# A prefix log-sum-exp scan: seven of eight batches in a hardware loop, four tile buffers, and a last tile loaded whole

## Chip, cores and metric

The kernel runs on one core of one Trainium2 chip. The metric is the device time of one execution in microseconds (us). A profile of one execution comes with it; its span goes from the first to the last instruction and is a little shorter than the device time.

## What is computed

The input is float32 of shape 8 x 4096 x 2048: eight batches, 4096 positions, 2048 channels. Along the positions each output is the running log of the sum of exponentials:

```
out[:, 0, :] = x[:, 0, :]
for t in range(1, S):
    mx = maximum(out[:, t-1, :], x[:, t, :])
    out[:, t, :] = mx + log(exp(out[:, t-1, :] - mx) + exp(x[:, t, :] - mx))
```

The kernel computes it as the log of a running sum of exp(x), without the maximum. Each batch is a scan of its own.

## The kernel before

A tile is 512 positions of one batch with all 2048 channels, 4 MiB; eight tiles (k = 0 to 7) make a batch, 64 the whole input. Partition p of a tile holds four successive positions (r = 0 to 3), and these lie one after the other in memory, so that the tile is 32 KiB in a row for each of the 128 partitions, in one DMA (L76). A tile is worked on in four pieces of 512 channels (c = 0 to 3). Python loops write all 256 pieces out; there is no branch in the program.

For each piece `front` has the ScalarE engine (ACT) take Exp of all four positions into bf16 (L88). Four matmuls with triangular masks sum over partitions into a PSUM bank (L91). VectorE (DVE) copies the bank (L96) and adds the positions r = 1 to 3 one after the other (L98); the result is `st`. `carry` multiplies the last row of `st` with the mask `last`, and so puts the running total of the tile into the bank of the next tile of the same batch (L103). `back` takes Ln of `st`, on ACT, and writes it over the input in the tile's buffer (L110). After the fourth piece the tile leaves in one DMA, issued by ACT (L114).

The order on each engine is the order in which the code is written: front of piece n, carry of piece n-1, back of piece n-2 (LAG = 2). So on ACT the last two Ln of a tile, and its store behind them, stand behind the first two Exp of the next tile, across batches too. Loads are issued by the SP queue, stores by the ACT queue. The pool `iopool` has five buffers for tiles (L52). A load is written ahead of all work of its tile, and it waits on SP until the store of the tile that had the buffer before has landed.

The last of the 64 tiles is an exception: it is loaded in four DMAs, one per piece (L74), each with 2 KiB in a row, and stored in four (L112). The masks are made at the start by GpSimd (POOL).

Of the kernel before, what the change touches and what calls it, by code (L numbers as in the profile page):

```python
# [1 line left out]

# [4 lines left out]


@with_exitstack
def kernel(  # L10
    ctx: ExitStack,
    tc: tile.TileContext,
    x: bass.AP,
    out: bass.AP,
):

    nc = tc.nc
    f32 = mybir.dt.float32
    bf16 = mybir.dt.bfloat16
    ACT = mybir.ActivationFunctionType
    nc.scalar.preload_act_table_set("natural_log_exp_and_others")  # L29

    B, S, D = x.shape
    P = 128
    R = 4
    NBLK = S // (P * R)
    FD = 512
    NC = D // FD
    LAG = 2

    const = ctx.enter_context(tc.tile_pool(name="const", bufs=1))
    Li = const.tile([P, P], bf16)  # L40
    masks.make_upper_triangular(nc, Li, val=1.0, diag=True)
    Ls = const.tile([P, P], bf16)
    masks.make_upper_triangular(nc, Ls, val=1.0, diag=False)

    last = const.tile([P, P], f32)
    nc.gpsimd.memset(last, 1.0)  # L46
    nc.gpsimd.affine_select(  # L47
        out=last, in_=last, compare_op=mybir.AluOpType.is_ge, fill=0.0,
        base=-(P - 1), pattern=[[0, P]], channel_multiplier=1,
    )  # L50

    iopool = ctx.enter_context(tc.tile_pool(name="iopool", bufs=5))  # L52
    epool = ctx.enter_context(tc.tile_pool(name="epool", bufs=4))
    spool = ctx.enter_context(tc.tile_pool(name="spool", bufs=3))
    ppool = ctx.enter_context(tc.tile_pool(name="ppool", bufs=2, space=bass.MemoryType.PSUM))

    x_v = x.rearrange("b (k p r) d -> b k p r d", p=P, r=R)
    o_v = out.rearrange("b (k p r) d -> b k p r d", p=P, r=R)

    tiles = [(b, k) for b in range(B) for k in range(NBLK)]  # L60
    pieces = [(b, k, c) for b, k in tiles for c in range(NC)]
    io = {}
    sums = {}
    banks = {}

    def cols(c):
        return slice(c * FD, (c + 1) * FD)

    def load(b, k):
        t = iopool.tile([P, R, D], f32, name=f"io_{b}_{k}", tag="io")  # L70
        io[b, k] = t
        if (b, k) == tiles[-1]:
            for c in range(NC):
                nc.sync.dma_start(out=t[:, :, cols(c)], in_=x_v[b, k][:, :, cols(c)])  # L74
        else:
            nc.sync.dma_start(out=t, in_=x_v[b, k])  # L76

    def bank(b, k, c):
        if (b, k, c) not in banks:
            banks[b, k, c] = ppool.tile([P, FD], f32, name=f"ps_{b}_{k}_{c}", tag=f"ps{c}")  # L80
        return banks[b, k, c]

    def front(b, k, c):
        if c == 0:
            load(b, k)
        t = io[b, k]
        et = epool.tile([P, R, FD], bf16, name="et")
        nc.scalar.activation(et, t[:, :, cols(c)], ACT.Exp)  # L88
        ps = bank(b, k, c)
        for r in range(R):  # L90
            nc.tensor.matmul(  # L91
                ps, Li if r == 0 else Ls, et[:, r, :],
                start=(k == 0 and r == 0), stop=(r == R - 1), skip_group_check=True,
            )
        st = spool.tile([P, R, FD], f32, name="st")
        nc.vector.tensor_copy(st[:, 0, :], ps)  # L96
        for r in range(1, R):
            nc.vector.tensor_add(st[:, r, :], st[:, r - 1, :], et[:, r, :])  # L98
        sums[b, k, c] = st

    def carry(b, k, c):
        if k < NBLK - 1:
            nc.tensor.matmul(  # L103
                bank(b, k + 1, c), last, sums[b, k, c][:, R - 1, :],
                start=True, stop=False, skip_group_check=True,
            )

    def back(b, k, c):
        t = io[b, k]
        nc.scalar.activation(t[:, :, cols(c)], sums.pop((b, k, c)), ACT.Ln)  # L110
        if (b, k) == tiles[-1]:
            nc.scalar.dma_start(out=o_v[b, k][:, :, cols(c)], in_=t[:, :, cols(c)])  # L112
        elif c == NC - 1:
            nc.scalar.dma_start(out=o_v[b, k], in_=t)  # L114

    for n, piece in enumerate(pieces):
        front(*piece)
        if n >= 1:
            carry(*pieces[n - 1])
        if n >= LAG:  # L120
            back(*pieces[n - LAG])
    for piece in pieces[-LAG:]:
        back(*piece)


# [1 line left out]
_INS = ['x']  # L127
_OUTS = [((8, 4096, 2048), 'float32')]


# [23 lines left out]
```

## Time and profile before

| What | Value |
|---|---|
| Time, median of 10 runs | 1259.64 us (1259.51 to 1259.86) |
| The profiled execution's own time | 1259.65 us |
| Its span | 1257.9 us |
| ACT busy | 930.0 us (74%), 513 instructions |
| DVE busy | 703.6 us (56%) |
| TensorE busy | 643.7 us (51%) |
| DMA | 537.22 MB, mean 427 GB/s over the span |
| HBM read and written | 268.44 MB each |

The profile's page gives the span in 40 slices of equal length. In them a digit is the busy share of an engine in tenths, and a number is the rate of all 16 DMA engines of the core in GB/s. A group line has: line, engine, operation, tiles written and read, shapes and count; then its busy time and the mean duration of one in ns; then the idle time of the engine just before such instructions and what ended it. A DMA line ends with the size of one DMA and the median time from issue to landing. In the queue's own waits, the three numbers are the time in total, how often, and the longest.

### The profile page before, as it was taken

The page shows a single profiled execution, that of the slowest core. Times are in us where ns is not written, and L with a number is a line of the kernel's source. Part 1 is how long each engine was busy: PE and PEld are TensorE (multiplying, and loading weights), DVE is VectorE, ACT ScalarE, POOL GpSimd, SP SyncE. Part 2 cuts the span into 40 slices and gives each one's busy share as a digit, 9 for nine tenths or more (in the row PEclk, how much of TensorE's full clock was granted, in tenths as well). Part 3 has the DMA queues.
Part 4 walks back from the last instruction along what each step waited for, and adds up shares of the span by engine and source line. Part 5 has one row for each costly group of instructions (what it writes and reads, how often), then busy time and mean ns, then how long its engine had stood idle before and what let it go on. Part 6 is the DMA issues. An engine that isn't in the chain of part 4 may idle for free.

```text
span 1257.9 us, 5492 instructions
## 1 busy us (share of the span) xinstructions
PE 643.7 (51%) x1472; PEld 215.9 (17%) x1472; DVE 703.6 (56%) x1024; ACT 930.0 (74%) x513; POOL 1.5 (0%) x10
## 2 busy tenths in 40 slices
PE   4655446554555455554555545455555455454542
PEld 1211112111111111111111111111111111111110
DVE  3766556555565554655555656565465555655453
ACT  5987768668677686776867768678687686776665
POOL 0000000000000000000000000000000000000000
PEclk9888577776787857878578786787767877678695
DMA  9999999999999999999999999999999999999997
GB/s 401 426 431 433 433 432 430 432 432 434 433 434 432 431 433 432 433 431 433 432 433 433 432 433 433 433 433 433 434 432 433 434 433 431 433 433 433 433 382 299
DMA packets 22399, 537.22 MB, mean 427 GB/s; under 512 B 2144, under 2 KB 2144, under 8 KB 6240
## 3 DMA queue, kind: packets, MB, share of 16 engines
q1 hardware_dynamic: 11184, 268.44, 49.7%
q10 hardware_dynamic: 11184, 268.44, 49.6%
q8 instruction: 11, 0.18, 0.1%
q14 instruction: 20, 0.16, 0.0%
HBM read 268.44 MB, written 268.44 MB: 427 GB/s over the span
## 4 chain that ended last, share of the span: by engine, by line
DMA 72%; ACT 15%; issue 5%; DVE 3%; PE 3%; SPq 1%; ACTq 0%; DVEq 0%
DMA io<-in_x_dram 69%; ACT io L110 9%; ACT et L88 6%; DVE st L98 2%; DMA out_dram<-io 2%; PE ps L91 2%; PE ps L103 1%; DVE st L96 1%; SPq L74 1%; ACTq L114 0%; ACTq L110 0%; ACTq L88 0%; DVEq L98 0%; DVEq L96 0%; SPq L76 0%
## 5 line engine op out<-in xcount | busy, mean ns | idle before, releaser
L88 ACT ACTIVATE et<-io 128x2048 bf16<-128x2048 f32 x256 | 485.3, 1897 | 302.9 <-DMA io<-in_x_dram 302.9
L98 DVE TENSOR_TENSOR st<-st,et 128x512 f32<-128x512 f32 x768 | 531.0, 692 | 43.4
L110 ACT ACTIVATE io<-st 128x2048 f32<-128x2048 f32 x256 | 484.6, 1894 | 13.3 <-DMA io<-in_x_dram 10.7
L96 DVE COPY st<-ps 128x512 f32<-128x512 f32 x256 | 176.8, 690 | 498.0 <-PE ps L91 492.9
L103 PE MATMUL ps<-st,last 128*128 128x512 f32 x448 | 309.0, 779 | 135.6 <-DVE st L98 134.5
L91 PE MATMUL ps<-et,Li 128*128 128x512 bf16 x256 | 125.7, 491 | 462.7 <-ACT et L88 461.1
L91 PE MATMUL ps<-et,Ls 128*128 128x512 bf16 x768 | 288.2, 498 | 0.0
L91 PEld LDWEIGHTS <-Ls 128*128 128x128 bf16 x768 | 89.7, 117 | 695.2 <-issue 666.1
L103 PEld LDWEIGHTS ps<-st,last 128*128 128x128 f32 x448 | 95.1, 237 | 250.2 <-DVE st L98 227.7
L91 PEld LDWEIGHTS <-Li 128*128 128x128 bf16 x256 | 31.1, 121 | 79.7 <-issue 72.7
L29 ACT ACT_TABLE_LOAD x1 | 1.3, 1283 | 0.8 <-PEq L138 0.8
L47 POOL TENSOR_SCALAR_AFFINE_SELECT last<-last 128x128 f32<-128x128 f32 x1 | 0.3, 292 | 0.1
masks.py:66 POOL TENSOR_SCALAR_AFFINE_SELECT Li<-Li 128x128 bf16<-128x128 bf16 x1 | 0.3, 292 | 0.0
masks.py:66 POOL TENSOR_SCALAR_AFFINE_SELECT Ls<-Ls 128x128 bf16<-128x128 bf16 x1 | 0.3, 292 | 0.0
masks.py:65 POOL MEMSET Li<- 128x128 bf16 x1 | 0.2, 204 | 0.3 <-POOLq L138 0.3
masks.py:65 POOL MEMSET Ls<- 128x128 bf16 x1 | 0.2, 204 | 0.0
L46 POOL MEMSET last<- 128x128 f32 x1 | 0.2, 204 | 0.0
L138 POOL MEMSET const-bfloat16-1.0<- 128x1 bf16 x1 | 0.1, 102 | 0.0
L138 POOL MEMSET const-uint8-127<- 128x1 uint8 x1 | 0.1, 102 | 0.0
L138 POOL MEMSET const-float32-0.0<- 128x1 f32 x1 | 0.1, 98 | 0.3 <-issue 0.3
L138 POOL MEMSET const-float32-1.0<- 128x1 f32 x1 | 0.1, 98 | 0.0
## 6 DMA issues: line engine op xcount, KB each, us to landing
io<-in_x_dram SPq DMA_DIRECT2D x63, 4096.0 KB, 31.4
out_dram<-io ACTq DMA_DIRECT2D x63, 4096.0 KB, 38.5
io<-in_x_dram SPq DMA_DIRECT2D x4, 1024.0 KB, 39.5
out_dram<-io ACTq DMA_DIRECT2D x4, 1024.0 KB, 10.3
```

The costliest lines, as they stand in the source:

```text
L29: nc.scalar.preload_act_table_set("natural_log_exp_and_others")
L46: nc.gpsimd.memset(last, 1.0)
L47: nc.gpsimd.affine_select(out=last, in_=last, compare_op=mybir.AluOpType.is_ge, fill=0.0, base=-(P - 1), pattern=[[0, P]], channel_multipl ...
L74: nc.sync.dma_start(out=t[:, :, cols(c)], in_=x_v[b, k][:, :, cols(c)])
L88: nc.scalar.activation(et, t[:, :, cols(c)], ACT.Exp)
L91: nc.tensor.matmul(ps, Li if r == 0 else Ls, et[:, r, :], start=(k == 0 and r == 0), stop=(r == R - 1), skip_group_check=True,)
L96: nc.vector.tensor_copy(st[:, 0, :], ps)
L98: nc.vector.tensor_add(st[:, r, :], st[:, r - 1, :], et[:, r, :])
L103: nc.tensor.matmul(bank(b, k + 1, c), last, sums[b, k, c][:, R - 1, :], start=True, stop=False, skip_group_check=True,)
L110: nc.scalar.activation(t[:, :, cols(c)], sums.pop((b, k, c)), ACT.Ln)
L138: nc = _bacc.Bacc("TRN2", target_bir_lowering=False, num_devices=1)
```

## The change

Batches one to seven become the body of a hardware loop, `tc.For_i(0, B - 1, 1, iteration_sync="reg_based")`; batch eight is written out after it. The body is one batch, eight tiles written out as before, and the batch's number comes from a register, in the DRAM address of every load and store. The loop construct, by its own description, does not reset its semaphores between iterations: they only increase, and a wait in the body compares with a register that is raised at each iteration. The semaphores belong to the loop alone; they are raised by one iteration's ticks ahead of it and cleared in its exit block.

The pieces of one batch are now a list of their own: the last two `back` of a batch come at its end and no longer behind the first two `front` of the next batch. The pool of tile buffers has four instead of five. The last tile is loaded by the same DMA as every other. Its results leave in three DMAs: channels 0 to 1023 after the second piece, then one per piece. Exp, matmuls, sums and Ln are the same. The diff, cut to its core:

```diff
-    iopool = ctx.enter_context(tc.tile_pool(name="iopool", bufs=5))
+    iopool = ctx.enter_context(tc.tile_pool(name="iopool", bufs=4))
...
-    def load(b, k):
-        t = iopool.tile([P, R, D], f32, name=f"io_{b}_{k}", tag="io")
-        io[b, k] = t
-        if (b, k) == tiles[-1]:
-            for c in range(NC):
-                nc.sync.dma_start(out=t[:, :, cols(c)], in_=x_v[b, k][:, :, cols(c)])
-        else:
-            nc.sync.dma_start(out=t, in_=x_v[b, k])
...
+    def batch(b, final):
+        pieces = [(k, c) for k in range(NBLK) for c in range(NC)]
+        io, sums, banks = {}, {}, {}
+        xb = x_v[b] if isinstance(b, int) else x_v[bass.ds(b, 1)][0]
+        ob = o_v[b] if isinstance(b, int) else o_v[bass.ds(b, 1)][0]
...
+        def front(k, c):
+            if c == 0:
+                io[k] = iopool.tile([P, R, D], f32, name=f"io{k}", tag="io")
+                nc.sync.dma_start(out=io[k], in_=xb[k])
...
+        def back(k, c):
+            nc.scalar.activation(io[k][:, :, cols(c)], sums.pop((k, c)), ACT.Ln)
+            if final and k == NBLK - 1:
+                if c > 0:
+                    part = slice(0 if c == 1 else c * FD, (c + 1) * FD)
+                    nc.scalar.dma_start(out=ob[k][:, :, part], in_=io[k][:, :, part])
+            elif c == NC - 1:
+                nc.scalar.dma_start(out=ob[k], in_=io[k])
+
+        for n, piece in enumerate(pieces):
+            front(*piece)
+            if n >= 1:
+                carry(*pieces[n - 1])
+            if n >= LAG:
+                back(*pieces[n - LAG])
+        for piece in pieces[-LAG:]:
+            back(*piece)
+
+    with tc.For_i(0, B - 1, 1, iteration_sync="reg_based") as b:
+        batch(b, False)
+    batch(B - 1, True)
```

More of the change, by code (lines that the diff above doesn't have):

```diff
@@ L58 @@
     o_v = out.rearrange("b (k p r) d -> b k p r d", p=P, r=R)
[L60 to L64, printed above, removed]
     def cols(c):
         return slice(c * FD, (c + 1) * FD)
-    def load(b, k):
-        t = iopool.tile([P, R, D], f32, name=f"io_{b}_{k}", tag="io")
-        io[b, k] = t
-        if (b, k) == tiles[-1]:
-            for c in range(NC):
-                nc.sync.dma_start(out=t[:, :, cols(c)], in_=x_v[b, k][:, :, cols(c)])
-        else:
-            nc.sync.dma_start(out=t, in_=x_v[b, k])
@@ L78, in bank @@
[L78 to L123, printed above, removed]
+    def batch(b, final):
[3 more added lines that the diff above has]
+        ob = o_v[b] if isinstance(b, int) else o_v[bass.ds(b, 1)][0]
+        def bank(k, c):
+            if (k, c) not in banks:
+                banks[k, c] = ppool.tile([P, FD], f32, name=f"ps{k}_{c}", tag=f"ps{c}")
+            return banks[k, c]
+        def front(k, c):
+            if c == 0:
+                io[k] = iopool.tile([P, R, D], f32, name=f"io{k}", tag="io")
+                nc.sync.dma_start(out=io[k], in_=xb[k])
+            et = epool.tile([P, R, FD], bf16, name="et")
+            nc.scalar.activation(et, io[k][:, :, cols(c)], ACT.Exp)
+            ps = bank(k, c)
+            for r in range(R):
+                nc.tensor.matmul(
+                    ps, Li if r == 0 else Ls, et[:, r, :],
+                    start=(k == 0 and r == 0), stop=(r == R - 1), skip_group_check=True,
+                )
+            st = spool.tile([P, R, FD], f32, name="st")
+            nc.vector.tensor_copy(st[:, 0, :], ps)
+            for r in range(1, R):
+                nc.vector.tensor_add(st[:, r, :], st[:, r - 1, :], et[:, r, :])
+            sums[k, c] = st
+        def carry(k, c):
+            if k < NBLK - 1:
+                nc.tensor.matmul(
+                    bank(k + 1, c), last, sums[k, c][:, R - 1, :],
+                    start=True, stop=False, skip_group_check=True,
+                )
+        def back(k, c):
[14 more added lines that the diff above has]
+            back(*piece)
```

## Prediction

> **What bounds the kernel now.** I read the page's slices first, then the queue's own waits, then the groups.
>
> ```profile
> span 1257.9 us, 5492 instructions
> DMA  9999999999999999999999999999999999999997
> GB/s 401 426 431 433 433 432 430 432 432 434 433 434 432 431 433 432 433 431 433 432 433 433 432 433 433 433 433 433 434 432 433 434 433 431 433 433 433 433 382 299
> L88 ACT ACTIVATE et<-io 128x2048 bf16<-128x2048 f32 x256 | 485.3, 1897 | 302.9 <-DMA io<-in_x_dram 302.9
> io<-in_x_dram SPq DMA_DIRECT2D x63, 4096.0 KB, 31.4
> out_dram<-io ACTq DMA_DIRECT2D x63, 4096.0 KB, 38.5
> io<-in_x_dram SPq DMA_DIRECT2D x4, 1024.0 KB, 39.5
> out_dram<-io ACTq DMA_DIRECT2D x4, 1024.0 KB, 10.3
> ```
>
> The DMA engines are full in every slice but the ends, at 433 GB/s. 536.87 MB at 433 is 1239.9 us; the other 18.0 us of the span are holes at the start and the end. One tile is 4.194 MB in and 4.194 MB out, 9.69 us each way, so the period is 19.4 us a tile. ACT waits only for loads. The queue's own waits say what a load waits for:
>
> ```profile
> SPq L76 <- DMA out_dram<-io: 1144.1, 58, 53.1
> ```
>
> A load waits until a store has emptied its buffer, never for an engine's work. Last, the windows of the end (their last columns are clock, DMA share and GB/s) and the issues from 1190 us on:
>
> ```profile
> 1220.00:1225.00 5.00, 0.00 (x0) 0.00 (x0) 0.40 (x1) 0.00 (x0) 0.00 (x0) 0.53 0.56 237
> 1225.00:1230.00 5.00, 0.68 (x2) 0.26 (x2) 0.00 (x0) 2.64 (x2) 0.00 (x0) 0.50 0.72 227
> 1230.00:1235.00 5.00, 4.42 (x9) 1.48 (x8) 3.21 (x5) 5.00 (x4) 0.00 (x0) 0.60 0.09 36
> ...
> DMA packets 4753, 23.48 MB, mean 345 GB/s; under 512 B 195, under 2 KB 195, under 8 KB 4291
> ```
>
> From 1190 us to the end 23.48 MB move; at 433 they need 54.2 us of the 67.9, so **13.7 us are lost at the end**. The hole from 1220 to 1235 alone loses (196+206+397) x 5 / 433 = 9.2 us. The last tile is still coming in 2 KiB pieces while no store is queued: its four loads take 36 to 42 us each, and store 62 cannot leave, since ACT reaches the last two Ln of tile 62 only behind two Exp of tile 63.
>
> **What the Trainium skill says.** "DMA: Bandwidth & Descriptors", section "Queues, rings and completion order": an engine takes turns between queues packet by packet. So a queue of 2 KiB pieces beside one of 32 KiB pieces gets few bytes. The trace agrees: from 1190 us on the loads moved 4.42 MB and the stores 19.04. The same page, "Anatomy of one DMA — SWDGE (gpsimd) path": about 2 us of each DMA are fixed, most of it the receipt of the last write. That is measured for another issuing path than SP's; the first load here lands in 12.38 us, 2.7 over its 9.69. "Advanced Engine Details and Errata", "Control Flow Timing": a compare and branch is about 108 ns; the kernel before has no branch. "Runtime: NRT & Kernel Launch", "Instruction fetch mechanics": a branch out of the fetched window stalls for a fetch; no size is given and no run here shows it.
>
> **The change, part by part.**
>
> Last tile as one load of 32 KiB pieces, results in three parts. It now shares evenly with the stores and lands as every load does. Let it land at T. Two Exp and two Ln precede store 62; the trace has such a store 7.3 us after the first Exp (1143.05 to 1150.39). When T comes, the stores left are down to what remains of store 61. By the bookkeeping of the exit below this ends at T+6, and its gap to store 62's first byte (1.2 us after issue, part of the fixed 2.7) is some 2.3 us. Store 62 streams from T+8.5 to T+18.2; the parts of tile 63 are issued at about T+14.5, T+17 and T+20 (ACTIVATEs every 1.8 us, and 1.4 us for the last sum as in the profile), so nothing else is empty. Four MB in pieces of 2 and 4 KiB at about 386 (as the last slices of before go) instead of 433 cost 1.2 us, receipt and closing 2.2. Loss 5.7 instead of 13.7: **-8.0 us** (bounds -5 to -10).
>
> Four io buffers for five. A buffer's round is 5 x 19.4 = 97 us now: load 31.4, work about 27 until the store's issue, store 38.5. Four give 77.5. What a round needs at least is 12.4 + 27 + 12 = 51 us; the rest is queueing. Loads and stores then spend about 25 us each, and still between one and three transfers wait. **0 us**; the cover is this 26 us of queueing, and it would cost only beyond that.
>
> The loop's edges, six of them. The option named in the diff lets the semaphores only grow and compares each wait with a register raised once per iteration; nothing halts all engines there. SP's first load of a batch then waits for the store of tile 4 of the batch before, as it would written out (8 tiles over 4 buffers keep the same slots). ACT loses the interleaving: the last two Ln of a batch come before the first Exp of the next. That lets the last store of a batch leave without the next load, and may stand about 1.4 us for the last sum. ACT has 4.84 us idle per tile (its wait at 1143 us). Branch 0.1 us, register updates and perhaps a fetch of some us lie in the same idle and in the 26 us. **0 us** (bounds 0 to 2 per edge).
>
> Register work ahead of waits and DMA addresses taken from a register: no row shows it. SP has idle to spare. ACT issues a store in 0.34 us; a doubling fits in the 4.84 us. **0 us**; it counts once ACT gets over 4.84 / 8 = 0.6 us more per ACTIVATE.
>
> Entry of the loop. The first load is issued at 0.81 us now. Before it come register writes, the raising of the loop's semaphores, and perhaps a meeting of the engines behind POOL's masks, which end at 2.2 us. **+2 us** (bounds 0 and 4), all on the path: nothing is in flight yet.
>
> Exit of the loop, once, between batches seven and eight. The loop's semaphores are cleared there, and that can only be done when every DMA of the loop has landed. So batch eight's first load, on SP, waits for the last store of batch seven, and SP has eight loads queued behind. Let T be the landing of the loop's last load (tile 55). It was issued some 25 us before T, when store 51 landed; store 52 landed a period later, at T-5.6, its last bytes at about T-7. So store 53 has had half the rate for 7 us, 1.5 MB, and its other 2.7 MB end at T+6.2; 54 is issued at T+7.3 and first moves at T+8.5: gap 2.3. It ends at T+18.2; 55 is issued at T+20 (ten ACTIVATEs of 1.8, the last sum and the issue) and moves at T+21.2: gap 3.0. It ends at T+30.9; receipt 1.2, a meeting of the engines, issue to first byte 1.5. For the meeting the profile has a price, the kernel's own end:
>
> ```profile
> L149 SPq DRAIN  x3: 7/7/7, 1257.2 to 1257.5; - x3
> L149 POOLq EVENT_SEMAPHORE_RANGE_CLEAR  x1: 96/96/96, 1257.5 to 1257.5; - x1
> L149 ACTq EVENT_SEMAPHORE  x2: 17/17/17, 1257.4 to 1257.9; - x2
> ```
>
> Meet, clear, meet again in 0.7 us; I take 1.1. Gap 3.8. After it four loads are issued at once and store 56 follows before they run out, so nothing more is lost. **+9.1 us** for the gaps (bounds 5 to 12) and **+0.5** for what else the exit executes (0 to 4).
>
> Sum: 1257.9 - 8.0 + 2.0 + 9.1 + 0.5 = 1261.5 us of span. The profiled execution took 1259.65, 1.75 over its span and 0.01 from the median of 1259.64. So **1263.2 us**. The bounds together, not all bad at once, give 1255 to 1271.
>
> **The rivals.**
> No drain at the exit, or a short one: the later batch's loads pass the exit while stores still run. For it: those loads need nothing but free buffers. Against: the clearing. It gives 1259.6 - 8 + 2 = 1253.6.
> The iterations do not overlap: the first load of a batch waits for the last store of the batch before, because the tracking across iterations is coarse or a barrier comes after all. Six edges more of 9.1 us are 55: 1318. It decides when the wait of a batch's first load is on tile 7's store and not tile 4's. Nothing in the profile excludes it; the slots dividing evenly speak against it.
> Stores with a register in their address are ordered one behind another: ACT would hold each store until the one before has landed, 19.4 us at a half share plus 2.2 (the shortest store takes 11.9 for 9.7 us of bytes), so a period of 21.6 for 19.4 in 55 tiles: about +120, 1383.
> Waits through registers slow ACT beyond its idle: 0.65 us per ACTIVATE is 0.05 x 8 x 56 = 22 us, 1285.
>
> **How the numbers follow.** Forecast 0.68, of which faster 0.06, within 0.2% (2.5 us, about what a measurement of this kernel can tell from no change: 1257.1 to 1262.2) 0.32 and slower 0.30, since 1263.2 lies close above that bound. No drain 0.08; no overlap 0.12; ordered stores 0.06; slow waits 0.06. Faster 0.14, same 0.32, slower 0.54. The forecast's own range is 1255 to 1271. For eight in ten, no drain and most of slow waits come in: 1252 to 1290 holds about 0.81. The forecast lies near no change because two sums of 8 and 9 us cancel, not because little happens.
>
> **What would show it.** GB/s stays near 433 at each batch edge before the last, one dip with some 9 us of holes lies between 1065 and 1105 us, the hole at 1220 to 1235 is gone, and the first load is issued at 2 to 4 us. Loads and stores take about 25 us each. Dips every 155 us would mean no overlap; a shorter ACT idle everywhere, slow waits; an even flow with no dip, no drain. I am wrong if the drain's gaps are not about as long as the hole that the end loses.

## The result and the profile after

The changed kernel takes 1441.6 us (median of 8 runs) against 1259.7 us (median of 28): a ratio of 1.1446, 95% interval 1.1436 to 1.1456. The forecast was 1263.2 us, with eight chances in ten between 1252 and 1290. The side was right (slower had 0.54), but for another reason than the forecast gave, and the size was not: 182 us where 3.6 were forecast.

The page of the kernel after, the lines that answer to those of before; a group line ends with the idle time ahead of it and its releaser, a DMA line with its median time to landing:

```profile
span 1442.2 us, 7727 instructions
GB/s 393 375 344 394 356 364 384 352 393 362 370 374 354 392 363 366 378 349 393 360 382 364 349 393 361 392 353 362 380 346 390 354 378 364 335 389 422 430 428 310
L101 ACT ACTIVATE io<-st 128x2048 f32<-128x2048 f32 x256 | 485.0, 1898 | 363.6 <-DMA out_dram<-io 332.9
io<-in_x_dram SPq DMA_DIRECT2D x64, 4096.0 KB, 22.5
out_dram<-io ACTq DMA_DIRECT2D x63, 4096.0 KB, 22.6
```

The rate is no longer 433 GB/s but swings about 370, all through the loop and evenly, so there is no single hole to look for. It is back at 422 to 430 in slices 37 to 39, which are batch eight, outside the loop. The duration of an ACTIVATE is as before (1898 ns, before 1894). What is new is the releaser: ACT, in its own Ln groups, stood 332.9 us for the landing of **stores**. In the kernel before the only DMAs that it waited for were loads.

One tile in the middle, in order of time (start, duration, engine, line):

```profile
440.80 0.33 SPq L78 DMA_DIRECT2D io<-in_x_dram  x1
440.81 0.36 ACTq L108 DMA_DIRECT2D out_dram<-io  x1
441.28 1.91 ACT L101 ACTIVATE io<-st 128x2048 f32<-128x2048 f32 x1 [8.22 <-DMA out_dram<-io]
```

A load and a store leave 10 ns apart; over the next ten tiles the two are never more than 0.1 us apart. Windows of the same tile (the last two columns are DMA share and GB/s):

```profile
440.00:443.00 3.00, 0.00 (x0) 0.00 (x0) 0.00 (x0) 1.72 (x1) 0.00 (x0) 0.50 0.84 175
443.00:446.00 3.00, 0.96 (x3) 0.40 (x3) 0.00 (x0) 3.00 (x3) 0.00 (x0) 0.50 0.81 350
...
461.00:463.50 2.50, 0.29 (x1) 0.00 (x0) 0.00 (x0) 0.00 (x0) 0.00 (x0) 1.00 0.49 210
```

The DMA engines run low at the start and at the end of the tile. The period is 22.65 us: ACT's last store of a batch is at 191.19 us and two batches later at 553.61, so 362.4 us for 16 tiles. Both transfers land some 22.6 us after their issue, 3.2 more than the 19.4 us that their bytes need together. The packets of the trace show where the 3.25 us of a period go: between two tiles no packet runs on any DMA engine for 1.6 us (median of 44 tiles; in the middle of the kernel before this never happens), the first packet on each engine then takes 2.4 us (median) where the others take 1.2, and the sixteen engines end a transfer some 0.6 us apart.

This gives the theory. The dependency tracker is the part of the framework that decides which instruction waits for which. In the compiled program of the loop each store waits, besides its Ln, on the semaphore of the store of the tile before; batch eight's stores and those of the kernel before do not. The store's address comes from a register, and the tracker keeps two such stores to the same tensor in order. So a store goes out when the one before has landed. The same landing frees a buffer and releases a load. **Load and store start together, end together, and nothing is queued behind them**: the fixed part of a DMA, which was hidden under other transfers, lies bare once per tile. Rivals: register work slows the engines; iterations do not overlap; four buffers are too few; or it is the holding of ACT, not the single store, that costs.

### The profile page after: what moved, and what is told of

It reads as the page before. It is cut to its first block, busy times and chain, and to the rows that moved or that the text cites. A ratio compares the mean times of both kernels' runs of the same rounds, so it can differ in the third digit from the quotient of the medians.

```text
span 1442.2 us, 7727 instructions
## 1 busy us (share of the span) xinstructions
PE 653.0 (45%) x1472; PEld 211.4 (15%) x1472; DVE 696.5 (48%) x1024; ACT 932.1 (65%) x513; POOL 1.5 (0%) x10
## 5 line engine op out<-in xcount | busy, mean ns | idle before, releaser
L101 ACT ACTIVATE io<-st 128x2048 f32<-128x2048 f32 x256 | 485.0, 1898 | 363.6 <-DMA out_dram<-io 332.9
L80 ACT ACTIVATE et<-io 128x2048 bf16<-128x2048 f32 x256 | 482.5, 1894 | 133.1 <-issue 75.6
L95 PE MATMUL ps<-st,last 128*128 128x512 f32 x448 | 297.6, 752 | 144.4 <-DVE st L90 143.7
L83 PE MATMUL ps<-et,Ls 128*128 128x512 bf16 x768 | 300.7, 515 | 0.0
L95 PEld LDWEIGHTS ps<-st,last 128*128 128x128 f32 x448 | 88.5, 223 | 264.2 <-DVE st L90 227.1
## 6 DMA issues: line engine op xcount, KB each, us to landing
io<-in_x_dram SPq DMA_DIRECT2D x64, 4096.0 KB, 22.5
out_dram<-io ACTq DMA_DIRECT2D x63, 4096.0 KB, 22.6
```

The source lines that it names most:

```text
L80: nc.scalar.activation(et, io[k][:, :, cols(c)], ACT.Exp)
L83: nc.tensor.matmul(ps, Li if r == 0 else Ls, et[:, r, :], start=(k == 0 and r == 0), stop=(r == R - 1), skip_group_check=True,)
L95: nc.tensor.matmul(bank(k + 1, c), last, sums[k, c][:, R - 1, :], start=True, stop=False, skip_group_check=True,)
L101: nc.scalar.activation(io[k][:, :, cols(c)], sums.pop((k, c)), ACT.Ln)
```

## Experiments

**1. The loop with stores that are not ordered.** The output is seen through eight views, that is, eight names for the same memory, which the tracker takes as disjoint, one per tile of a batch.

```diff
-    o_v = out.rearrange("b (k p r) d -> b k p r d", p=P, r=R)
+    o_w = [v.rearrange("b (k p r) d -> b k p r d", p=P, r=R) for v in dram_disjoint_views(out, 8)]
...
-        ob = o_v[b] if isinstance(b, int) else o_v[bass.ds(b, 1)][0]
+        ob = [(o_w[k % 8][b] if isinstance(b, int) else o_w[k % 8][bass.ds(b, 1)][0])[k] for k in range(NBLK)]
```

Expected:

> The changed kernel with the output seen through eight views of the same memory, one per tile of a batch, which are declared disjoint, so that no store is ordered behind the store of another tile. Loop, register waits, four buffers and last tile stay. If the loss is each store waiting for the landing of the one before (ordered stores): about 1263 us, as the prediction had it without that wait, 1257 to 1270. If register work ahead of each wait slows ACT, or four buffers are too few: still above 1400 us. If iterations do not overlap: about 1318 us, with a hole every 155 us.

Measured: 1277.0 us (1274.3 to 1281.1), ratio 1.0139, interval 1.0124 to 1.0154. Of the 182 us, 165 go with the wait. Slow register waits, too few buffers and missing overlap fall as causes of these 165: loop, registers, branches and four buffers are all still there. 7 us more than the top of the range remain to be found. ACT's waits at the store's line, in the kernel after (L108) and in this one (L109), differ by 56, one for each store of the loop; below them the slices of this kernel:

```profile
L108 ACTq EVENT_SEMAPHORE  x70: 17/17/38, 29.1 to 1262.3; - x70
L109 ACTq EVENT_SEMAPHORE  x14: 17/17/17, 29.3 to 976.9; - x14
GB/s 381 425 425 434 434 431 432 437 431 429 437 432 430 435 434 431 432 437 431 430 437 431 430 434 434 431 428 429 429 426 419 430 429 330 348 426 426 428 427 303
```

The six inner edges (about every 5 slices) leave no dip. The one dip, 330 and 348, is the exit.

**2. Two stores in flight.** Two views, taken in turn (`8` becomes `2` in the diff above).

> The changed kernel with two disjoint views of the output, taken in turn by the tiles: a store waits for the store before last, so that two can be in flight. If the loss is one store at a time: the store before last left some 39 us earlier and needs some 27, so nothing waits, about 1277 us as with eight views. If any wait on an earlier store holds ACT: between 1300 and 1440 us.

Measured: 1275.7 us (1273.2 to 1277.1), as with eight views. A second store in flight is enough.

**3. The wait alone, without a loop.** In the kernel before:

```diff
-            nc.scalar.dma_start(out=o_v[b, k], in_=t)
+            ins = nc.scalar.dma_start(out=o_v[b, k], in_=t)
+            if prev:
+                tc.add_manual_dep(ins.ins, prev[-1].ins.name, mybir.DependencyInfo(
+                    mybir.DependencyClass.Sync, mybir.DependencyReason.DATA), reason="one store at a time")
+            prev.append(ins)
```

> The kernel before with one thing added: each store of a whole tile waits on ACT until the store before has landed. Ordered stores: the period grows from 19.4 to the 22.65 us that the changed kernel shows, in 62 tiles, so about 1460 us (1420 to 1480). Slow register waits or too few buffers as the cause: the wait alone costs little, below 1300 us.

Measured: 1466.7 us (1465.1 to 1467.4), ratio 1.164, interval 1.1623 to 1.1657. ACT now stands at the same place as in the kernel after:

```profile
ACT io L111 <- DMA out_dram<-io: 498.1, 59, 9.9
```

The wait makes the loss by itself, and the fifth buffer of the kernel before does not help: another buffer does not fill the gap when every release comes from the same landing.

**4. Who is held?** The stores of whole tiles go out from GpSimd, first free, then ordered as in 3. ACT then never waits for a store.

```diff
-            nc.scalar.dma_start(out=o_v[b, k], in_=t)
+            nc.gpsimd.dma_start(out=o_v[b, k], in_=t)
```

> The kernel before with the stores of whole tiles issued by GpSimd instead of ACT; a base for the next run. The order of the stores is free: about 1260 us, up to 1280 if this path to the DMA engines is slower.

> Stores issued by GpSimd, each waiting there for the landing of the one before, so that one store is in flight at a time but ACT is never held. If the loss comes from holding ACT: below 1290 us. If it comes from load and store being released by the same landing and running in step, with the fixed part of both bare once a tile: about 1460 us, as when ACT waits (1430 to 1500).

Measured, one execution each: 1258.7 and 1460.5 us. With ACT free the loss is the same within some 6 us, so it does not come from the holding of ACT. In the ordered kernel's trace loads leave at 610.69, 633.23 and 656.27 us, and stores at 611.18, 633.71 and 656.75: in step again, 22.5 to 23 us apart. The ordered kernel's only waits of ACT for a DMA, and the times to landing on its page:

```profile
ACT et L89 <- DMA io<-in_x_dram: 502.5, 61, 11.0
io<-in_x_dram SPq DMA_DIRECT2D x63, 4096.0 KB, 20.4
out_dram<-io POOLq DMA_DIRECT2D x63, 4096.0 KB, 22.3
```

**5. The parts beside the loop.** Four kernels separate the last tile, the buffers and the order of the pieces.

The last tile alone (kernel before, L72 to L76 cut to the whole load, the three partial stores):

> The kernel before with only the last tile changed: one load of 32 KiB pieces, results in three parts, five buffers. 8 us less than before by the prediction's step: 1251.6 us (1249.5 to 1254.6), whatever holds the loop.

Batches written out, with all else of the change:

```diff
-    with tc.For_i(0, B - 1, 1, iteration_sync="reg_based") as b:
+    for b in range(B - 1):
         batch(b, False)
```

> The changed kernel with a Python loop over batches one to seven in place of the hardware loop: addresses are constants, four buffers, the batch-wise order of the pieces and the whole last tile stay. Ordered stores or slow register waits: both end at 1251.6 us (1259.6 less the 8 us of the end), since the loop is gone. Four buffers too few: above 1400 us.

The kernel before with `bufs=4`:

> The kernel before with four tile buffers in place of five, nothing else. The batches written out with four buffers took 1272.4 us where the whole last tile alone took 1257.2, so 15 us hang on the buffers or on the batch-wise order. If on the buffers: 1272 to 1277 us, with the rate in the middle sinking below 430 GB/s. If on the order of the pieces, or if the prediction's zero for the buffers holds: 1259 to 1261 us.

Batches written out with `bufs=5`:

> The batches written out, whole last tile and batch-wise order of the pieces as in the change, but five buffers. If the 15 us hang on the buffers: about 1257 us, as with the whole last tile alone. If on the batch-wise order: about 1272 us.

| Kernel | Buffers | Measured, us | Ratio to before, interval |
|---|---|---|---|
| last tile whole | 5 | 1257.2 (1256.8 to 1257.6) | 0.9979 (0.9970 to 0.9987) |
| written out | 4 | 1272.4 (1266.0 to 1275.1) | 1.0089 (1.0070 to 1.0108) |
| before with 4 | 4 | 1267.8 (1260.0 to 1272.5) | 1.0063 (1.0038 to 1.0088) |
| written out | 5 | 1256.9 (1256.6 to 1257.9) | 0.9978 (0.9970 to 0.9986) |

The last tile alone gained less than its range allowed, and neither kernel with four buffers fell into a range that was named for it; the last one did (buffers, not order). With five buffers the batch-wise order costs nothing, and both kernels beat the one before by 2.5 to 2.8 us. Four buffers cost 8 us on top of the kernel before and 15 on top of the written-out one, and they scatter by 9 and 12 us where five scatter by about 1. Writing the batches out takes the loop and the registers away together, so these runs do not say on which of the two the tracker's order hangs. The rate of the written-out kernel with four, whose middle sinks and does not come back:

```profile
GB/s 405 419 427 430 434 432 434 432 433 422 436 432 430 430 432 428 430 428 426 420 427 426 418 428 413 427 426 430 429 417 427 427 418 431 426 417 441 420 423 271
```

The packets of the traces point to a reason. Each DMA of a tile ends with sixteen small packets, which I take as one per DMA engine, and the time from the first to the last of them says how far apart the engines have drifted. In the kernel before it grows from 0.8 us at the first load to some 10 us at the last whole ones, and the rate stays at 433. With four buffers it grows too, but for the loads it stops at about 10 us, and there the rate begins to sink. In the written-out kernel most loads have 9 us of spread by 400 us and 9.5 to 11 from 600 on; it loses 0.6 us in each 100 us from 300 to 500 and 1.6 to 2.6 from 600 on. In the profiled run of the kernel before with four, a fast one, the loads get there only at about 900 us; it loses 0.3 us from 600 to 900 and 3.3 from 900 to 1190. It would follow that the engines that are ahead run out of queued packets, while the last one keeps the buffer from coming free. This fits the traces, but no run tests it, and why the engines drift is open.

**6. The price of an edge.** The loop with eight views, but with the barrier that is the construct's default (`iteration_sync="barrier"`):

> Eight views and four buffers, but the loop stops every engine between iterations (the construct's default). Six more drains like the one at the exit, which lost 13.3 us in the loop with eight views: 1277 + 6 x 13.3 = 1357 us (1330 to 1370); with the prediction's 9.1 us an edge 1332.

Measured: 1328.0 us (1324.5 to 1328.9). Six more edges cost 51 us, 8.5 each, near the 9.1 of the prediction's step and just below the range. In this kernel's trace each edge, the exit too, loses 8.3 to 9.3 us, where the exit of the loop without barriers lost 13.3: here the engines are at most 2.7 us apart at an edge, there 10 us in the last load and 13.5 in the stores before the exit.

**7. The loop with five buffers** (`bufs=5` in the kernel of 1):

> The loop with eight views and five buffers in place of four. Each iteration gives its tiles the same buffers, so the first three loads of a batch wait for the stores of tiles 5, 6 and 7 of the batch before, three tiles back instead of four. If the fifth buffer matters only for the middle's rate: 1277 less the 4 us that the middle loses with four buffers and less some of the exit's 13 us, 1265 to 1273 us. If the shorter distance at each edge starves the DMA engines: dips every 155 us, 5 to 8 us each, 1300 to 1325 us.

Measured: 1278.5 us (1277.5 to 1279.2), in neither range. Dips at the edges are there but shallow (slices at 401, 393, 404). From 64 to 1050 us this kernel loses 18 us, where the one with four buffers loses 4; from there to the end it loses 12, where that one loses 25. So the edges eat what the exit and the end gain, and in this loop four and five buffers come out alike.

## Why the prediction was wrong, step by step

**The loop's stores.** The step that failed is the sentence that a doubling of ACT's store issue "fits in the 4.84 us. **0 us**": it priced the address from a register as work and not as an order between stores. What the runs showed in its place: the order itself, 3.25 us a tile, 165 us in all (experiments 1 and 3). The ordered stores stood among the rivals at 0.06, with 1383 us. The mechanism was named rightly there, the size was not. That rival took 2.2 us for the fixed part, the least any store needs over its bytes; the chip showed 22.65 - 19.4 = 3.25. With 3.25 its sum would have been 1263.2 + 55 x 3.25 = 1442; that this meets the 1441.6 is partly luck, since three other terms of the sum were off by some 4 us each, as shown below. And the rival put the wait on ACT, where experiment 4 has the same loss with ACT never waiting for a store. Over the 1126 us from 64 to 1190 the kernel after moves 416.3 MB; at 433 this is 961.4 us, so 164.6 us are lost in 49.7 tiles of 22.65 us, 3.3 a tile. The two spans differ by 184.3 us; the other 20 lie in the start, the loop's last tiles with the exit, and the end. The Trainium skill's "DMA: Bandwidth & Descriptors", "Anatomy of one DMA — SWDGE (gpsimd) path", gives about 2 us for the fixed part of one DMA on that path; bare, in this kernel, it is 3.3 us for the pair. The low chance was a misjudgment that the profile could not have put right: the kernel before has no address from a register. The compiled program would have shown the wait.

**The rest of the sum**, read from the loop with eight views against the kernel before. Lost is the length of a stretch less its bytes at 433 GB/s:

| Stretch | Before, us lost | Loop, eight views | Forecast of the difference | Found |
|---|---|---|---|---|
| 0 to 64 (entry) | 3.0 | 4.6 | +2.0 | +1.6 |
| middle | 0.5 | 3.4 to 1050, 1.4 from 1110 to 1190 | 0 | +4.3 |
| exit, 1050 to 1110 | | 13.3 | +9.6 | +13.3 |
| end, from 1190 | 13.7 | 10.2 | -8.0 | -3.5 |

**Entry**: right; the first load is issued at 2.25 us, forecast 2 to 4. **Inner edges**: right, 0; from 64 to 600 us the loop loses 0.3 us, and the windows around the three later edges lose 0.0 to 0.3 each. **Four buffers**: wrong. The step counted 26 us of queueing as cover and found 0; the chip gives 8 to 15 us without a loop, 4 within it. It took the sixteen DMA engines as one; that they come to lie some 10 us apart may be what used up the cover. **Exit**: right mechanism, one term too small. Windows of the kernel of experiment 1 around it:

```profile
1072.00:1076.00 4.00, 0.36 (x1) 0.10 (x1) 0.47 (x1) 2.32 (x2) 0.00 (x0) 0.73 0.31 131
1076.00:1080.00 4.00, 3.97 (x8) 1.39 (x7) 2.22 (x4) 4.00 (x3) 0.00 (x0) 0.50 0.06 25
1080.00:1084.00 4.00, 1.97 (x7) 0.69 (x6) 3.32 (x6) 4.00 (x3) 0.00 (x0) 0.92 0.62 262
...
1092.00:1096.00 4.00, 0.00 (x0) 0.00 (x0) 0.00 (x0) 1.35 (x1) 0.00 (x0) 0.50 0.63 266
...
1104.00:1108.00 4.00, 0.00 (x0) 0.10 (x1) 0.00 (x0) 0.00 (x0) 0.00 (x0) 0.50 0.53 164
```

The three holes of the forecast are all there: before store 54, before store 55, and before the next loads. The first loses 8.1 us where 2.3 were forecast: when tile 55 had landed at 1073.7 us, store 53 had 0.23 MB left and not 2.7. Fifteen of its sixteen end packets had come by 1075.7, the last came at 1080.5. By then the engines had drifted apart: those that were done with tile 55's load had gone on with store 53, and the landing waited for the last one. The others lose 2.4 (forecast 3.0) and 2.5 (3.8). From the last landing to the next load are 0.5 us (1104.6 to 1105.09), so the meeting of the engines was rather too dear at 1.1.

**The end**: right direction, mis-sized. The last tile alone gains 2.5 us, not 8. Windows of that kernel's end:

```profile
1220.00:1225.00 5.00, 1.57 (x4) 0.75 (x4) 0.43 (x1) 3.53 (x2) 0.00 (x0) 0.56 0.76 328
1225.00:1230.00 5.00, 3.20 (x7) 0.90 (x6) 4.29 (x7) 5.00 (x4) 0.00 (x0) 0.76 0.35 151
1230.00:1235.00 5.00, 2.48 (x6) 0.81 (x6) 3.62 (x6) 5.00 (x4) 0.00 (x0) 0.58 0.98 419
...
1250.00:1255.40 5.40, 0.00 (x0) 0.00 (x0) 0.00 (x0) 0.00 (x0) 0.00 (x0) 0.50 0.08 32
```

The hole before store 62 loses 1.2 + 3.3 = 4.5 us and not 2.3, the same term as at the exit; the last load's end packets are 10 us apart here too. And the last 5.4 us move almost nothing: 32 GB/s is 5.0 us lost where 2.2 were taken for receipt and closing. The old hole of 9.2 us is gone, but the end still loses 11.2 us against 13.7, and these two are 9.5 of them.

In two places the prediction's own working is loose. The 4.42 MB of loads against 19.04 of stores, given as the trace's agreement with the turns between queues, are what was left to move from 1190 us on; a stretch in which both queues were busy, 1200 to 1210 us, says it better: 0.66 MB of loads, 3.21 MB of stores. And it takes 1.2 us from issue to first byte at the stores but 1.5 after the exit.

Of the 17 us that the loop with eight views stays above before, some 2 lie outside its span (1277.0 less 1273.1 is 3.9; before it is 1.75). Where they are the profile does not say; the kernel after has 1.45.

## What to carry to other kernels

When addresses move into registers, look in the compiled program for what each DMA now waits on: two writes to one tensor that were plainly apart may be put in order, and views declared disjoint undo that. A stream that is bound by DMA needs releases at different moments: if a load and a store are released by the same landing and nothing is queued behind them, the fixed part of a DMA is paid once per tile; here four or five buffers, and ACT or GpSimd as the waiting engine, made no difference to that. Count the transfers in flight, not only the time that buffers have to spare; without a loop the fifth buffer was worth 8 to 15 us and a steady time. Where all DMAs must land, at a loop's exit or a barrier, reckon with the last of the sixteen DMA engines and not with their mean.

## What the runs showed of the hardware that was not expected

An inner edge of this loop is cheap, its exit (13.3 us) is not. The compare and branch at an edge took 44 to 90 ns on ACT, SP and DVE and 221 ns (median) on TensorE's queue, each register step 29 to 93 ns, and six edges together left no hole. The Trainium skill's price of about 108 ns ("Advanced Engine Details and Errata", "Control Flow Timing") lies between the two. The DMA engines do not keep step: in the kernel before, the ends of one load lay 0.8 us apart at the start and some 10 us at the end; in the kernel after, where every tile of the loop waits for all of them, some 0.6. Stores issued from GpSimd were as good as from ACT here, 1258.7 us against 1259.9 in one execution each. With one tile buffer fewer, the kernel before scatters by 12 us from run to run.
